# A two-layer convolution and DeltaNet backbone: TensorE issued in program order, four heads scanned together

## The chip, the cores and the metric

The kernel runs on one core of a Trainium2 chip. The metric is the device time of one launch in microseconds (us); three runs of the kernel before gave 2870.46, 2883.15 and 2887.36 us, and their median of 2883.15 us is the time to beat or lose to. The profile is of another execution of the same program; its time is known as the span from its first to its last instruction.

The engines named below: PE (TensorE, matrix multiply), DVE (VectorE), ACT (ScalarE), POOL (GpSimd), and SP (SyncE), whose queue issues every DMA of this kernel. Each works through its own list of instructions in order, and waits at an instruction until what it needs is there.

## The reference

Two layers over 256 context and 2048 latent tokens of width 1024. Per layer, cut to what matters:

```python
h = rms_norm(x, norm_w) * (1 + scale) + shift          # scale, shift, gate from silu(c) @ w_mod + b_mod
p = h @ w_in                                           # 1024 -> 4112 columns, float32
# group A: gated short convolution
ya = bg * conv(cg * xa) * silu(za)
# group B: q, k, v = silu(conv(.)), l2 norms, write gate beta, decay g; 4 heads of 128
a_mat = strict(beta * (k @ k.T) * decay)               # per chunk of tokens
sol = triangular_solve(a_mat + I, [v * beta, k * beta * exp(gcum)])
# scan over the chunks, forward and backward, latent scans start from the context's final state
u = u0 - w @ S
S = S * exp(g_last) + k_dec.T @ u
o = q_dec @ S + p_intra @ u
yb = rms_norm(o_forward + o_backward) * silu(zb)
x = x + gate * (concat(ya, yb) @ w_out)
```

The second layer's context is only read; after it comes a last `rms_norm`.

## The kernel before

**Tiling.** Tokens are 18 tiles of 128 (0 and 1 context, 2 to 17 latent), in chunks: chunk 0 is the context (256 tokens), chunks 1 to 4 are 512 latent tokens each. Float32 products are made of three passes: a tensor is split into a rounded part and a rest (`whi` and `wlo` of the weights, `h` and `l` of the tokens; `hc` and `lc` for chunk 0), and `project` (L272) sums `h·whi`, `l·whi` and `h·wlo` over 8 slices of the contraction. It does so in two halves of 256 columns (L276 to L278), each half with all 24 passes. One unit is 128 output columns: its weights are loaded (512 KB), rounded on ACT (L251) and subtracted on POOL (L253). A projected unit is consumed by ACT and DVE: convolution, SiLU, store to DRAM.

**Stages of a layer.** `prep` (L215) turns a chunk's normalised tokens channel-major: PE transposes into a PSUM bank (L225), ACT evicts with the modulation into `hf` (L231), DVE and POOL split it. In the same loop L240 projects the 16 gate columns in plain float32. Chunks 0 to 2 are also kept in DRAM (L233). `phase` runs units over chunks: q, k, v of the context, then of chunks 1 and 2, then 3 and 4; then the other units of 3 and 4; then those of 1, 2 (and 0), reloaded. `delta` (L476) takes one head's 16 latent tiles: per item it reloads the tile, transposes q, k, v (L495), makes `k·[k q]` (L511) and multiplies by the decays into `U` (L512); then it inverts the triangular blocks (31 elimination steps of two DVE instructions, L573 and L575) and assembles them on PE (L601 to L638). Then the same head's scan runs (`step`, L666): forward and backward step by step in turn, each a chain PE L684 (`k·S`), DVE L686 (`r`), PE L689 (`V·r`), DVE L692 (`wk`), PE L694, DVE L703 (new state), with L712 and L713 for the output. Each step loads its operands (256 KB, L674), and its triangle masks are applied on POOL out of `U`, which stays in SBUF (L678, L709). The four heads come one after the other beside the units of chunks 3 and 4.

**Order.** Every engine's list, PE's among them, is set by a scheduler that simulates the program and takes at each moment the most urgent instruction whose inputs it believes ready; `urgent()` raises the priority. So scan matmuls, item matmuls and projection passes are interleaved one by one.

## Time and profile before

| | |
|---|---|
| timed runs | 2870.46, 2883.15, 2887.36 us |
| span of the profiled execution | 2868.8 us |
| PE busy | 2740.4 us (96%) |
| DVE, ACT, POOL busy | 1794.5, 1139.6, 1002.2 us |
| mean granted TensorE clock | 0.982 |
| DMA queue, share of 16 engines | 53.7% |

The profiled execution is known by its span alone; the median of the runs is 14.35 us longer, the fastest run 1.7 us. "Busy" of PE counts pipelined matmuls with modelled ends, so a busy PE can still issue at different rates; how far apart matmuls start is the better measure. The granted clock is 1.00 at 2.4 GHz and 0.5 at 1.2 GHz.

### The profile page before, as it was taken

How to read it: one execution, taken by the hardware profiler on the slowest of the kernel's cores; microseconds unless marked ns; L12 is line 12 of the kernel's file. 1: busy time of each engine (PE TensorE's matmuls, PEld its weight loads, DVE VectorE, ACT ScalarE, POOL GpSimd, SP SyncE). 2: the span in 40 equal slices, each digit the busy share in tenths (PEclk: the TensorE clock that was granted, in tenths of full speed). 3: DMA queues.
4: the chain of work that ended last, by engine and by line, in shares of the span. 5: the costliest groups of instructions: out<-in, count | busy, mean ns of one | idle time of the engine just before them, and what ended most of it. 6: DMA issues, size and time to landing. Idle time of an engine off the chain costs nothing. (4 is left out here: it accounts for less than half of the span.)

```text
span 2868.8 us, 62580 instructions
## 1 busy us (share of the span) xinstructions
PE 2740.4 (96%) x23671; PEld 2529.1 (88%) x23671; DVE 1794.5 (63%) x4677; ACT 1139.6 (40%) x2962; POOL 1002.2 (35%) x1354
## 2 busy tenths in 40 slices
PE   7999999999999999999999999999999998999998
PEld 5799899988988999997777998899999888899887
DVE  5686657576586585353246776675766765754765
ACT  3544453533534532232115444435335354322332
POOL 2332322333433343234444222313334333333443
PEclk9999999999999999999999999999999999999999
DMA  8844265553655553347757552545546556434654
GB/s 275 251 120 138 81 174 130 174 162 89 182 145 170 173 139 113 109 149 246 239 161 242 162 144 79 154 112 163 154 115 188 132 168 189 126 116 118 206 173 117
DMA packets 589449, 450.17 MB, mean 157 GB/s; under 512 B 105322, under 2 KB 527196, under 8 KB 589148
## 3 DMA queue, kind: packets, MB, share of 16 engines
q1 hardware_dynamic: 589148, 446.16, 53.7%
q8 instruction: 188, 3.08, 0.4%
q14 instruction: 113, 0.93, 0.1%
HBM read 326.35 MB, written 119.70 MB: 155 GB/s over the span
## 5 line engine op out<-in xcount | busy, mean ns | idle before, releaser
L278 PE MATMUL pd<-h,whi 128*128 128x256 f32 x4096 | 1206.6, 295 | 2.1 <-ACT whi L251 2.1
L278 PE MATMUL pd<-l,whi 128*128 128x256 f32 x4096 | 1207.2, 295 | 0.0
L278 PE MATMUL pd<-h,wlo 128*128 128x256 f32 x4096 | 1199.4, 293 | 0.5 <-POOL wlo L253 0.5
L278 PEld LDWEIGHTS pd<-h,whi 128*128 128x128 f32 x4096 | 795.2, 194 | 11.9 <-issue 6.6
L278 PEld LDWEIGHTS pd<-l,whi 128*128 128x128 f32 x4096 | 795.0, 194 | 9.0 <-issue 5.4
L278 PEld LDWEIGHTS pd<-h,wlo 128*128 128x128 f32 x4096 | 794.8, 194 | 6.4 <-issue 2.9
L253 POOL TENSOR_TENSOR wlo<-raw,whi 128x1024 fp32r<-128x1024 f32 (+1 forms) x148 | 341.3, 2307 | 382.3 <-ACT whi L251 349.7
L899 PE MATMUL pd<-who,yy 128*128 128x512 f32 x1088 | 350.7, 397 | 0.4 <-ACT who L841 0.4
L899 PEld LDWEIGHTS pd<-who,yy 128*128 128x128 f32 x1088 | 203.6, 189 | 48.0 <-ACT yy L874 2.9
L697 ACT ACTIVATE w<-pscan,cs 128x128 f32<-128x128 f32 x272 | 99.5, 367 | 291.8 <-DVE wk L692 209.1
L899 PE MATMUL pd<-wlo,yy 128*128 128x512 f32 x544 | 214.1, 393 | 0.0
L251 ACT CAST whi<-raw 128x1024 fp32r<-128x1024 f32 x148 | 154.7, 1045 | 97.4 <-PE pd L278 60.9
L501 POOL TENSOR_TENSOR nk<-nk,phalf 128x1 f32<-128x1 f32 x144 | 81.7, 567 | 225.2 <-DVE nk L500 205.8
L573 DVE TENSOR_TENSOR tmp<-L,X 64x31 f32<-64x31 f32 (+15 forms) x310 | 127.1, 410 | 39.9 <-DMA L<-blk 25.0
L388 ACT ACTIVATE pd<-y 128x512 f32<-128x512 f32 (+1 forms) x116 | 65.5, 565 | 213.0 <-DVE y L288 200.6
L686 DVE SCALAR_TENSOR_TENSOR r<-pscan,eg,rc 128x128 f32<-128x128 f32 x272 | 93.7, 346 | 76.7 <-PE pscan L684 74.5
L575 DVE TENSOR_TENSOR X<-X,tmp 64x31 f32<-64x31 f32 (+15 forms) x310 | 136.3, 440 | 5.6
L692 DVE TENSOR_SCALAR wk<-pscan,cs 128x128 f32<-128x128 f32 x272 | 93.5, 346 | 69.6 <-PE pscan L689 67.7
L875 POOL TENSOR_TENSOR yy<-ys,yy 128x512 fp32r<-128x512 f32 x68 | 89.9, 1323 | 125.4 <-ACT yy L874 118.3
L660 POOL TENSOR_TENSOR so<-so,mhalf 128x1 f32<-128x1 f32 x136 | 79.2, 590 | 142.5 <-DVE so L659 134.3
L703 DVE SCALAR_TENSOR_TENSOR Sn<-Sn,atot,pscan 128x128 f32<-128x128 f32 x240 | 82.0, 342 | 67.9 <-PE pscan L694 66.6
L874 ACT CAST yy<-ys 128x512 fp32r<-128x512 f32 x68 | 42.1, 619 | 198.2 <-DVE ys L867 136.8
(2212 smaller groups left out, 5317.3 us busy)
## 6 DMA issues: line engine op xcount, KB each, us to landing
raw<-in_w_in_dram SPq DMA_DIRECT2D x148, 512.0 KB, 4.8
rc<-rec_d SPq DMA_DIRECT2D x272, 256.0 KB, 3.1
rec<-rec_d SPq DMA_DIRECT2D x136, 192.0 KB, 2.6
wm<-in_w_mod_dram SPq DMA_DIRECT2D x24, 1024.0 KB, 7.3
rec_d<-y SPq DMA_DIRECT2D x96, 256.0 KB, 2.9
rows<-row_d SPq DMA_DIRECT2D x144, 128.0 KB, 4.1
rec_d<-rec SPq DMA_DIRECT2D x144, 128.0 KB, 4.0
ys<-y_d SPq DMA_DIRECT2D x68, 256.0 KB, 3.5
```

Of the source, the lines that this page charges most:

```text
L251: nc.scalar.copy(hi, raw)
L253: eng.tensor_sub(lo[:, k], raw[:, k], hi[:, k].bitcast(F32))
L278: nc.tensor.matmul(acc[:, c:c + CW], w[i][:, k, :], h[j][:, k, c:c + CW], start=(z == 0), stop=(z == len(passes) - 1))
L501: nc.gpsimd.tensor_tensor(nk[:, i:i + 1], nk[:, i:i + 1], phalf[:, 0:1], ALU.pow)
L573: nc.vector.tensor_tensor(t3, L3[:, j + 1:32, j:j + 1].to_broadcast([2 * nb, m, k]), X3[:, j:j + 1, 0:k].to_broadcast([2 * nb, m, k]), ALU ...
L575: nc.vector.tensor_sub(X3[:, j + 1:32, 0:k], X3[:, j + 1:32, 0:k], t3)
L686: nc.vector.scalar_tensor_tensor(r, p1[:, 0:128], eg[:, g, col], vn, ALU.mult, ALU.subtract)
L692: nc.vector.tensor_scalar(wk, p2[:, 0:128], cs[:, 5 + z0 + d, i:i + 1], None, ALU.mult)
L697: nc.scalar.activation(w, p2[:, 0:128], AF.Copy, scale=cs[:, z0 + d, i:i + 1])
L703: nc.vector.scalar_tensor_tensor(Sn, S, atot[:, g, col], p3[:, 0:128], ALU.mult, ALU.add)
L875: nc.gpsimd.tensor_sub(l_, yr, h_.bitcast(F32))
L899: nc.tensor.matmul(acc, yy[k // 4][:, k % 4, :], wo[k][part][:, cs_], start=(z == 0), stop=(z == 23))
```

## The change

PE's list is no longer the scheduler's: it is the order in which the program emits instructions (`manual_schedule` for PE). The other engines are scheduled as before. The program is written as jobs (generators). `phase` emits projections, and after every three passes `pump` lets one due job emit a piece. A job that has emitted something says with `yield` how many microseconds of counted PE work are to go by before its next piece: 4.5 (`HOP`) between the links of a scan, 3.2 between items, 50 + 2 per item before the solved blocks are used, 1.3 between blocks of `prep`, and so on. `until` lets jobs emit without projections between when something named has to exist first.

The work changes too. `project` runs all 512 columns of a chunk in one matmul. The gate columns are projected in three-pass form (`two`). `delta` prepares two heads with 8 tiles each, and stores `U` to DRAM beside q, k, v. The scan is apart from it: one step takes all 4 heads of a tile, forward over all 16 tiles and then backward, its operands of 4 heads loaded in one transfer (128 x 3072 floats, 1536 KB, into a ring of two), masked in place on POOL; the backward pass adds the stored forward result. The scans of the latent tokens run beside the later units and the output projection. The edges of a phase with several chunks take three units chunk by chunk, so their weights are loaded once per chunk: 202 loads where there were 148. PSUM banks are fixed and taken in turn, and buffers come from rings; `hf` now has two buffers where it had four or five.

In the excerpts below PE's rows are in the order in which it issues them; a row with x4 is four such instructions. First a scan beside projections: the kernel before, in the first layer's units of chunks 1 and 2 or later (`pd` is a projection's bank, `pscan` a scan's).

```order
L278 MATMUL pd<-l,whi 128x256
L684 MATMUL pscan<-Sn,rc 128x128
L278 MATMUL pd<-h,wlo 128x256
L278 MATMUL pd<-h,whi 128x256
L278 MATMUL pd<-l,whi 128x256
L278 MATMUL pd<-h,wlo 128x256
L278 MATMUL pd<-h,whi 128x256
L662 MATMUL pscan<-ident,o_12043 128x128
L278 MATMUL pd<-l,whi 128x256
L694 MATMUL pscan<-wk,rc 128x128
L278 MATMUL pd<-h,wlo 128x256
L278 MATMUL pd<-h,whi 128x256
```

The change, two links of a scan step (`c_86` and `c_87` are the scan's banks, `d_81` and `d_82` a projection's):

```order
L149 MATMUL d_81<-h,whi 128x512
L149 MATMUL d_81<-l,whi 128x512
L149 MATMUL d_81<-h,wlo 128x512
L149 MATMUL c_86<-wk,rc 128x128 x4
L149 MATMUL c_87<-w,rc 128x128 x4
L149 MATMUL d_82<-h,whi 128x512
L149 MATMUL d_82<-l,whi 128x512
L149 MATMUL d_82<-h,wlo 128x512
L149 MATMUL d_82<-h,whi 128x512
```

Where single matmuls of one head stood among passes of 256 columns, four heads stand together among passes of 512; between the group before (`c_87<-r,rc`) and `c_86<-wk,rc` there are 24 projection rows, in the output stage mostly 21.

Second, where the first layer's q, k, v of chunks 1 and 2 end and chunk 3 is prepared (`xx` are its normalised tokens, `t_84`, `t_85` and `pt` the banks of transposes and items). Before, its transposes stand among projections:

```order
L278 MATMUL pd<-h,whi 128x256
L278 MATMUL pd<-l,whi 128x256
L278 MATMUL pd<-h,wlo 128x256
L278 MATMUL pd<-h,whi 128x256
L225 MATMUL pt<-ident,xx 128x128 x4
L689 MATMUL pscan<-rc,V__1719 128x128
L689 MATMUL pscan<-rc,V__1739 128x128
L278 MATMUL pd<-l,whi 128x256
L278 MATMUL pd<-h,wlo 128x256
L278 MATMUL pd<-h,whi 128x256
L278 MATMUL pd<-l,whi 128x256
```

In the change the last two projection rows of chunk 2 come first, and behind them items (`rec`) and the context's scan without a projection between:

```order
L149 MATMUL d_82<-l,whi 128x512
L149 MATMUL d_82<-h,wlo 128x512
L156 MATMUL t_84<-ident,rec 128x128 x3
L149 MATMUL t_85<-rec 128x256
L156 MATMUL t_84<-ident,rec 128x128 x3
L149 MATMUL t_85<-rec 128x256
L149 MATMUL c_87<-r,rc 128x128 x4
L156 MATMUL t_84<-ident,rec 128x128 x3
L149 MATMUL t_85<-rec 128x256
L149 MATMUL c_86<-wk,rc 128x128 x4
L149 MATMUL c_87<-w,rc 128x128 x4
L156 MATMUL t_84<-ident,rec 128x128 x3
```

This goes on to the end of the context's scan, and straight behind it come the blocks of chunk 3, eight in a row:

```order
L149 MATMUL c_86<-wk,rc 128x128 x4
L149 MATMUL c_87<-w,rc 128x128 x4
L156 MATMUL o_88<-ident,op 128x128 x8
L156 MATMUL t_84<-ident,xx 128x128 x4
L156 MATMUL t_85<-ident,xx 128x128 x4
```

Then chunk 3's projections begin. So from row 1068 to row 1100 of PE's list there is no projection.

The diff, cut to its core:

```diff
+HOP = 4.5
...
-    def stage(shape, n):
-        if n == 2:
-            return dp.tile(shape, F32, tag="rc", bufs=5, name="hf")
-        return dp.tile(shape, F32, tag="m2", bufs=4, name="hf")
...
+    def side(shape, name):
+        return dp.tile(shape, F32, tag="hf", bufs=2, name=name)
...
+    def mm(o, a, b, start=True, stop=True):
+        n = b.shape[-1]
+        nc.tensor.matmul(o, a, b, start=start, stop=stop)
+        if b.dtype == F32R:
+            Order.now += 0.0135 + n / 2400.0
+        else:
+            Order.now += 0.223 * n / 128 if n > 64 else 0.22 * n / 128 if a.shape[0] > 64 else 0.02
...
+    def spawn(name, gen):
+        Order.jobs.append([Order.now, gen, name])
+
+    def advance(job):
+        try:
+            d = next(job[1])
+            job[0] = Order.now + (d or 0.0)
+        except StopIteration:
+            Order.jobs.remove(job)
+            done.add(job[2])
+
+    def pump():
+
+        for job in Order.jobs:
+            if job[0] <= Order.now:
+                advance(job)
+                return
+
+    def until(what):
+
+        while what not in done:
+            job = min(Order.jobs, key=lambda j: j[0])
+            Order.now = max(Order.now, job[0])
+            advance(job)
 
     def vectors(l, P):
...
 
     def project(w, h):
-        W = h[0].shape[-1]
-        acc = pd()[:, 0:W]
-        passes = [(k, i, j) for k in range(KT) for i, j in ((0, 0), (0, 1), (1, 0))]
-        for c in range(0, W, CW):
-            for z, (k, i, j) in enumerate(passes):
-                nc.tensor.matmul(acc[:, c:c + CW], w[i][:, k, :], h[j][:, k, c:c + CW], start=(z == 0), stop=(z == len(passes) - 1))
+        acc = pd()[:, 0:h[0].shape[-1]]
+        for k in range(KT):
+            for z, (i, j) in enumerate(((0, 0), (0, 1), (1, 0))):
+                mm(acc, w[i][:, k, :], h[j][:, k, :], start=(k + z == 0), stop=(k + z == KT + 1))
+            if k < KT - 1:
+                pump()
         return acc
 
     def conv(dst, src, w, segs):
-        """dst = segment convolution of src, w the three per-channel weights."""
+
...
+            if xs is None:
+                xs = tokens_in(L, p)
+                yield 12.0
...
+                for k2 in range(0, KT, 2):
+                    ps = pt()
...
+                    hf = side([128, 2, 256], "hf")
...
+                    yield 1.3
+        done.add(("h", L.l, p))
...
+            yield 2.0
+            acc = pd()
+            for k in range(KT):
+                for j in range(2):
+                    mm(acc[0:96, 0:W], L.bw[:, 32 * k:32 * k + 96], L.hs[p][j][:, k, :], start=(k + j == 0), stop=(k + j == KT))
...
+    def phase(L, units, chunks, after, edge=3, ready={}):
+
+        N = len(units)
+        if len(chunks) == 1:
+            tasks = [(j, chunks[0]) for j in range(N)]
+        else:
+            tasks = [(j, p) for p in chunks for j in range(edge)]
+            tasks += [(j, p) for j in range(edge, N - edge) for p in chunks]
+            tasks += [(j, p) for p in chunks for j in range(N - edge, N)]
+        w = dict(ready)
+        left = {j: len(chunks) for j in range(N)}
+        of = {p: N for p in chunks}
+
+        def need(j):
+            if j < N and j not in w:
+                w[j] = weights(w_in[L.l], units[j][0], len(chunks) == 1)
+        for t, (j, p) in enumerate(tasks):
+            need(j)
+            wj = w[j] if t + 1 < len(tasks) and tasks[t + 1][0] == j else w.pop(j)
+            until(("h", L.l, p))
+            nxt = next((i for i, _ in tasks[t + 1:] if i != j), None)
+            if nxt is not None:
+                need(nxt)
+            a = project(wj, L.hs[p])
+            with urgent():
+                units[j][1](p, a)
+            left[j] -= 1
+            of[p] -= 1
+            for what, n in ((("unit", j), left[j]), (("chunk", p), of[p])):
+                if n == 0 and what in after:
+                    after[what]()
+            pump()
...
+            if i + 1 < n:
+                load(i + 1)
+            rec, rows = cur.pop(i)
+            with urgent():
                 tp = pt()
                 for s in range(s0, 3):
-                    nc.tensor.transpose(tp[:, 128 * s:128 * s + 128], rec[:, 3 - s, :], ident)
+                    turn(tp[:, 128 * s:128 * s + 128], rec[:, 3 - s, :])
+                kp = pt()
...
+            yield 3.2
+        held.discard("items")
...
+        yield 50.0 + 2.0 * n
...
+                    nc.sync.dma_start(out=L.rec_d[g:g + k, :, h, 512:512 + 128 * w_].rearrange("g p t -> p g t"),
+                                      in_=uz[:, j - i0:j - i0 + k, 0:w_, :].rearrange("p g s t -> p g (s t)"))
...
+                rc = dp.tile([128, NH, 6, 128], F32, tag="rc", bufs=2, name="rc")
+                if with_out:
+                    nc.sync.dma_start(out=rc.rearrange("p h s t -> p (h s t)"), in_=L.rec_d[g].rearrange("p h t -> p (h t)"))
...
+                for h in hd:
+                    m = rc[:, h, 4:4 + w_, :]
+                    nc.gpsimd.affine_select(out=m, in_=m, pattern=[[0, w_], [1 - 2 * d, 128]], compare_op=ALU.is_ge, fill=0.0, base=0, channel_multiplier=2 * d - 1)
...
+                    p1 = pscan("c0")
+                    for h in hd:
+                        mm(at(p1, h), kT[h], S[:, h, :])
+                    for h in hd:
+                        nc.vector.scalar_tensor_tensor(r[:, h, :], at(p1, h), e_(L.eg, h), vn[h], ALU.mult, ALU.subtract)
+                    if with_out:
+                        qs = pscan("o")
+                        for h in hd:
+                            mm(at(qs, h), qT[h], S[:, h, :])
...
+            yield HOP
+            with urgent():
+                p2 = pscan("c1")
+                for h in hd:
+                    mm(at(p2, h), V_[h], r[:, h, :])
+                wk = w4("wk")
+                for h in hd:
+                    nc.vector.tensor_scalar(wk[:, h, :], at(p2, h), cs(2 + d, h), None, ALU.mult)
...
+            yield HOP
+            with urgent():
+                p3 = pscan("c0")
+                for h in hd:
+                    mm(at(p3, h), kn[h], wk[:, h, :])
...
+                    pw = pscan("c1")
+                    for h in hd:
+                        mm(at(pw, h), P_[h], w[:, h, :])
...
+        def ready(g):
+            until(("y", l, g))
+            with urgent():
+                return mixed(g)
...
+        phase(L, [qkv_unit(L, s, h) for s, h in heads], (1, 2),
+              {("unit", 5): job(0), ("unit", 11): job(1), ("chunk", 1): lambda: spawn("p3", chunk_job(L, 3, False, z2))})
+        spawn("p4", chunk_job(L, 4, False, z2, last=True))
...
+        lat = list(range(2, NG))
+        w8 = {g: (f"J{l}3",) for g in range(10, NG)}
+        w8[2] = (f"J{l}1", f"C{l}0", f"C{l}1")
+        wb = {NG - 1: (f"F{l}0", f"J{l}3")}
+        spawn("lat", in_turn((f"F{l}0", alone("rc", scan(L, 0, lat, 0, wants=w8))), (f"F{l}1", alone("rc", scan(L, 1, lat[::-1], 1, wants=wb)))))
...
+    with tc.manual_schedule(engines={mybir.EngineType.PE}):
+        constants()
+        L = layers[0]
```

## Rows read from the trace of the kernel before

**Rows 1.** The page: busy us (share of the span) and instructions of each engine.

```profile
PE 2740.4 (96%) x23671; PEld 2529.1 (88%) x23671; DVE 1794.5 (63%) x4677; ACT 1139.6 (40%) x2962; POOL 1002.2 (35%) x1354
```

**Rows 2.** Span and mean granted TensorE clock of the core.

```profile
core 0: 2868.8 us, clock 0.982
```

**Rows 3.** Stretches with one kind of matmul: length, PE busy (matmuls), clock, DMA.

```profile
165.50:225.50 60.00, 60.00 (x502) 1.00 0.38 105
1498.70:1520.10 21.40, 21.40 (x96) 1.00 0.48 130
```

**Rows 4.** Timeline of PE in an output tile: start, length, matmuls.

```profile
1499.74 0.62 PE L899 MATMUL pd<-who,yy 128*128 128x512 f32 x2
1500.43 0.62 PE L899 MATMUL pd<-who,yy 128*128 128x512 f32 x2
```

**Rows 5.** PE groups: shapes, count | busy us, mean ns | idle before.

```profile
L278 PE MATMUL pd<-l,whi 128*128 128x256 f32 x4096 | 1207.2, 295 | 0.0
L240 PE MATMUL pt<-hf,braw 128*32 128x256 f32 x160 | 35.9, 390 | 0.3 <-ACT hf L231 0.3
L240 PE MATMUL pd<-hf,braw 128*32 128x256 f32 x128 | 30.6, 390 | 0.0
```

**Rows 6.** Timeline of PE: scan matmuls of one head amid projection.

```profile
1208.81 0.39 PE L694 MATMUL pscan<-wk,rc 128*128 128x128 f32 x2
1209.03 0.39 PE L713 MATMUL pscan<-w,P__11986 128*128 128x128 f32 x2
```

**Rows 7.** Waits of PE: us in total, times, longest.

```profile
PE pt L495 <- DMA rec<-rec_d: 20.0, 17, 3.6
PE pt L601 <- DMA tf<-blk: 14.2, 6, 3.4
PE pscan L684 <- DVE Sn L703: 14.0, 15, 2.8
PE pscan L689 <- DVE r L686: 11.4, 9, 3.3
PE pd L278 <- ACT whi L251: 5.0, 4, 2.1
PE pscan L684 <- DMA rc<-rec_d: 4.8, 2, 2.9
```

**Rows 8.** The page's costly groups on DVE, POOL and ACT.

```profile
L253 POOL TENSOR_TENSOR wlo<-raw,whi 128x1024 fp32r<-128x1024 f32 (+1 forms) x148 | 341.3, 2307 | 382.3 <-ACT whi L251 349.7
L251 ACT CAST whi<-raw 128x1024 fp32r<-128x1024 f32 x148 | 154.7, 1045 | 97.4 <-PE pd L278 60.9
L501 POOL TENSOR_TENSOR nk<-nk,phalf 128x1 f32<-128x1 f32 x144 | 81.7, 567 | 225.2 <-DVE nk L500 205.8
L686 DVE SCALAR_TENSOR_TENSOR r<-pscan,eg,rc 128x128 f32<-128x128 f32 x272 | 93.7, 346 | 76.7 <-PE pscan L684 74.5
```

**Rows 9.** Groups by line on ACT: a transposed block's eviction, and a token tile's squares.

```profile
L231 ACT ACTIVATE hf<-pscan,mod,am 128x256 f32<-128x256 f32 x80 | 40.1, 569 | 11.5 <-PE pscan L225 8.0 <-DVE am L150 1.4 <-issue 1.2
L183 ACT ACTIVATE junk<-xx 128x1024 bf16<-128x1024 f32 x28 | 29.8, 1065 | 36.3 <-DMA xx<-in_ctx_dram 23.4 <-DMA rec_d<-rec 4.9 <-DMA xx<-in_x_dram 3.4
```

**Rows 10.** DMA issues: count, KB each, median us to landing.

```profile
raw<-in_w_in_dram SPq DMA_DIRECT2D x148, 512.0 KB, 4.8
wm<-in_w_mod_dram SPq DMA_DIRECT2D x24, 1024.0 KB, 7.3
xx<-x SPq DMA_DIRECT2D x29, 512.0 KB, 4.9
h_d<-hf SPq DMA_DIRECT2D x36, 256.0 KB, 5.6
```

**Rows 11.** One line, the scan's triangle mask: ns minimum/median/maximum, first and last start.

```profile
L678 POOL TENSOR_SCALAR_AFFINE_SELECT V__1719<-U x1: 292/292/292, 250.2 to 250.2; 128x128 f32<-128x128 f32 x1
```

**Rows 12.** Timeline of DVE: last item of a head is prepared.

```profile
425.47 0.36 DVE L512 TENSOR_TENSOR U<-pt,dm 128x256 f32<-128x256 f32 x1
```

**Rows 13.** Timeline of PE: first matmul on that head's solved blocks.

```profile
497.31 0.25 PE L601 MATMUL pt<-tf,U 32*32 32x32 f32 x4 [3.18 <-DMA tf<-blk]
```

More of the change, by code (lines that the diff above doesn't have):

```diff
@@ new lines, in hybrid_backbone_kernel, with alone @@
+    class Order:
+        now = 0.0
+        jobs = []
+    done = set()
+    held = set()
+    def alone(what, gen):
+        while what in held:
+            yield 1.0
+        held.add(what)
+        yield from gen
+        held.discard(what)
+    def mm(o, a, b, start=True, stop=True):
[5 more added lines that the diff above has]
+            Order.now += 0.223 * n / 128 if n > 64 else 0.22 * n / 128 if a.shape[0] > 64 else 0.02
@@ L383, in consume, with mix_units, unit @@
+    def mix_units(L, a_, chunks):
+        par = L.P["par"]
+        cw = [par[:, 32 + 4 * j + a_:33 + 4 * j + a_] for j in range(3)]
+        t0 = {}
+        o = 0
+        for ci in chunks:
+            t0[ci] = o
+            o += 128 * CHUNKS[ci][1]
+        def unit(u):
             def consume(ci, a):
@@ L474, in layer @@
[L474 to L492 removed]
+                xs = xa[:, t0[ci]:t0[ci] + W]
@@ new lines, in delta, with load @@
+    def delta(L, items, with_out, before):
+        n = len(items)
+        heads = list(dict.fromkeys(h for h, _ in items))
+        nh, m = len(heads), n // len(heads)
+        h0, g0 = heads[0], items[0][1]
+        gs = slice(g0, g0 + m)
+        U = []
+        cur = {}
+        ssk = dp.tile([128, 16], F32, tag="ssk", bufs=2, name="ssk")
+        nk = dp.tile([128, 16], F32, tag="nk", bufs=2, name="nk")
+        s0 = 0 if with_out else 1
+        w_ = 2 if with_out else 1
+        def load(i):
+            with urgent():
+                h, g = items[i]
+                rec = small([128, 4, 128], "rec")
+                nc.sync.dma_start(out=rec[:, 1:4 - s0].rearrange("p s t -> p (s t)"), in_=L.rec_d[g, :, h, 128:512 - 128 * s0])
+                rows = dp.tile([128, 2, 128], F32, tag="rows", bufs=2, name="rows")
+                nc.sync.dma_start(out=rows, in_=L.row_d[8 * g + h:8 * g + h + 5:4].partition_broadcast(128))
+                cur[i] = rec, rows
+        while "items" in held:
+            yield 1.0
+        held.add("items")
+        load(0)
+        yield 6.0
+        for i, (h, g) in enumerate(items):
+            if i == 8 and before is not None:
+                while before not in done:
+                    yield 2.0
+            if i % 8 == 0:
+                U.append(dp.tile([128, 8, 2, 128], F32, tag="u", bufs=3, name="U"))
+            if i + 1 < n:
+                load(i + 1)
+            rec, rows = cur.pop(i)
+            with urgent():
@@ new lines, in hybrid_backbone_kernel @@
+    with tc.manual_schedule(engines={mybir.EngineType.PE}):
+        constants()
+        L = layers[0]
+        with urgent():
+            vectors(0, L.P)
+            xs0 = tokens_in(L, 0)
+            tables(L)
+            wm = []
+            for n in range(8):
+                if n % 2 == 0:
+                    wt = hp.tile([128, KT, 512], F32, tag="hl"[n // 2 % 2], bufs=2, name="wm")
+                wm.append(wt[:, :, CW * (n % 2):CW * (n % 2) + CW])
+                mod_load(0, wm[n], 2 * n)
+            for n in range(8):
+                for _ in mod_piece(0, L.P, wm[n], 2 * n):
+                    pass
+            mod_scale(0, L.P)
+        L.ready = {j: weights(w_in[0], qkv_unit(L, s, 0)[0], True) for j, s in enumerate((1, 2))}
+        spawn("p0", chunk_job(L, 0, True, {}, xs=xs0, last=True))
+        layer(L, layers[1])
+        until("next")
+        layer(layers[1], None)
```

1226 lines of the change are left out of this document (605 added, 621 removed).

## The prediction, made before the changed kernel ran

> **What bounds the kernel now.** I read the page's list of engines first: PE is busy 96% of the span and has four times as many instructions as the next engine [rows 1]. The view of the core shows the TensorE clock granted at 0.982 of full speed [rows 2]. So the kernel is bound by PE's list, and its time has three parts: what PE does, 128.4 us in which it idles (2868.8 - 2740.4) [rows 1, 2], and about 52 us that the clock kept back (0.018 x 2868.8) [rows 2]. A busy DVE or POOL matters only where PE waits for it.
>
> Then I looked at how far matmuls stand apart, in stretches that hold one kind alone. In 60 us of projection with 256 columns there are 502, 0.1195 us each; in 21.4 us of output projection with 512 columns there are 96, 0.223 each; both at clock 1.00 [rows 3]. The timeline has three 512-wide ones in 0.69 us, 0.23 each [rows 4]. I take 0.227 for a whole chunk, with 0.223 and 0.230 as ends. Two halves cost 0.239.
>
> Last, the waits. The six that cost PE most add up to 69.4 us: items that wait for their reload, solved blocks for their way through DRAM, and the links of a scan for DVE [rows 7].
>
> **The change part by part.** The base is the profiled execution's span, 2868.8 us; the median of the runs is 14.35 longer, and I add that at the end.
>
> Projection: three groups of 4096 matmuls, one of which is shown [rows 5], are 12288 halves x 0.1195 = 1468 us; 6144 whole ones x 0.227 = 1395. That is -74 (-55 at 0.230, -98 at 0.223).
>
> The Trainium skill ("TensorE: Matmul & The Clock Gate", section "Back-to-back issue gap") gives a warm matmul N/2.4 + 2.5 ns. By it a pair saves only the 2.5 ns, 6144 times 15 us, not 74. The rows here disagree: 119.5 ns is 12.8 above 256/2.4, so the part that does not grow with the columns is larger in this kernel than on that page [rows 3].
>
> Gate columns: 288 float32 matmuls are busy for 66.5 us [rows 5]. In three passes, run as two per slice, there are 128 of 512 columns and 32 of 256: 128 x 0.227 + 32 x 0.1195 = 33. That is -27, after some 6 for what they still stand beside (0 to -34).
>
> Scan matmuls: four heads in step need 16 more than before, counted in PE's list, at 0.22 each [rows 6]: +3.5.
>
> Waits that go: a scan's links come 21 or 24 projection passes apart, 21 x 0.227 = 4.8 us. The chain between them is a matmul of 0.39 [rows 6] and four DVE instructions of 0.346 [rows 8], 1.8 us. So DVE's part (14.0 + 11.4) goes. Items are loaded one ahead (20.0). Solved blocks are planned 82 us behind the last item; before they took from 425.47 to 497.31, 71.8 us [rows 12, 13], so 14.2 goes too, and so does 4.8 for `rc` [rows 7]. That is 64.4; smaller waits of these kinds lie in the rest of the 128.4. I take -75 (-30 if items and blocks stay late, -105 if nearly all idle time goes). L278's wait for rounded weights (5.0) stays.
>
> Clock: part of the 52 us follows such waits. I take -30 (0 to -45).
>
> What is late next are the borders where one chunk must be ready before PE has anything to project. Chunk 3's tokens share buffers with the context's scan, which ends directly ahead of them. Then come a token load of 4.9 [rows 10], two squares of 1.065 with the scaling behind them, about 3, and eight blocks of two evictions of 0.569, 9.1 [rows 9]. Of these 17 us some 7 lie beside the matmuls of items and scan: 10 a layer. Chunks 1 and 2 store each block from `hf`, a ring of two, and the store lands after 5.6 [rows 10]. Two blocks per 5.6 + 0.6 make 25 us for eight, where 10.4 are planned (8 x 1.3): 14 late per chunk. Projections of the chunk before cover most of it: I take 11 a layer. At the layers' border the gates' chain runs with little beside it: 15, from the same loads and evictions. Sum 2 x 10 + 2 x 11 + 15 = +57. Ends: 25 if the borders overlap with items, 140 if nothing covers them (2 x 17 + 4 x 14 + 50). A clock that falls in these gaps takes back +10 (0 to 40).
>
> Edges: the units that run chunk by chunk load 54 more weights (202 against 148), and then each weight serves 24 matmuls, 5.45 us. ACT rounds in 1.045 and POOL subtracts in 2.307 [rows 8], behind a load of 4.8 [rows 10], one unit ahead. Hidden in the mean, with POOL's queue behind it: I take +15 (0, to 54 x 3.36 = 181 if nothing hides ACT and POOL).
>
> Items and blocks take turns in two transpose banks, and an item comes every 3.2 us and more. Its chain through DVE and POOL (0.567 for one small POOL step [rows 8]) is about 2 us. 144 items give 0 to 144 us; I take +10, near the lower end, since a projection group lies between most of them. The stores of `U`, its reload and the masks moved to the load lie off PE's path unless the rival below holds.
>
> Sum: -74 - 27 + 3.5 - 75 - 30 + 57 + 10 + 15 + 10 = -110. The span becomes about 2758, and with 14.35 the time **2773**.
>
> **The rivals.** *The borders are covered.* The pieces that jobs emit between them may fill them, and edges and banks may cost nothing: -110 - 67 - 25, and 15 more from the clock, is -217, hence 2666. For it speaks that PE's order then has few stalls of any other kind; against it that some 30 of PE's rows at chunk 3 are emitted without a projection, and that blocks go at ACT's pace [rows 9].
>
> *The wide matmul gains nothing.* If the passes of whole chunks come 0.239 apart, the sum is -36 and the time 2847. Against it: the rows of 512 columns are the same kind of matmul at the same clock, with a DMA share of 0.48 beside 0.38 [rows 3, 4]. For it: they stand in the output projection, and no row shows a unit of `project` at that width.
>
> *The scan's operands come late (the other side).* A step loads 1536 KB into a ring of two. 512 KB land after 4.8, 1024 KB after 7.3 [rows 10], so 1536 KB after about 9.8. Then POOL masks four heads of 256 columns, 0.58 each by 0.292 for 128 [rows 11], 2.3, perhaps behind a `wlo` of 2.3 [rows 8]: 14.4 in all. A step lasts 3 x 4.8 + 22 x 0.22 = 19.2, and the buffer comes free only when the step before has ended. That leaves 4.8 to spare. If loads queue on SP behind weights and DRAM stores by 9 us, each of 64 latent steps (2 layers, 2 directions, 16) is 4 late: +256, 3029. From 124/64 = 1.9 us late per step on the kernel is slower than before by more than can be told from no change. For it: DMA rises by 202 weight loads and the reloads of `U`, and PE's order, being fixed, can no longer do something else meanwhile. Against it: before, the queue waited little for anything that PE needed (4.8 us for `rc` [rows 7]).
>
> *Waits come back at the two transpose banks and at the items.* At 0.7 us for each of 144 items, 100 more: the sum is about -10 and the time 2873, no change. For it: the 20.0 for items was the greatest wait before [rows 7], in a list that could put anything ahead of it. Against it: the planned distance is longer than the chain.
>
> **How the numbers follow.** Forecast 0.48, its own range 2710 to 2835 (the terms' ends taken together, not all on one side); borders covered 0.25; nothing from width 0.05; operands late 0.12; waits back 0.10. A difference of 0.5%, 14.4 us, is about what can be told from no change here, so faster means under 2868.7 and slower over 2897.6. The first three cases are faster, 0.78; the waits' case is the same, 0.10; late operands slower, 0.12. The range goes from 2640, near the low end of covered borders, to 2890, above the waits' case, and leaves out the late operands and the tail of the second case.
>
> **What would show it.** In the profile after: 6144 projection matmuls of 512 columns, 0.227 apart in a stretch that holds only these; two halves' 0.239 would prove the second rival. PE's waits at `k·S` and `V·r` for DVE near zero, and for items and `tf` under 10 us; if a wait for `rc` or for its mask leads the list, the third rival holds. Idle time of PE should stand in a few gaps of 5 to 20 us, at the first projection of chunks 1 to 3 of each layer and at the layers' border, behind ACT's block evictions or the `hf` stores; many short gaps at items and transposes mean the fourth. The clock should be near 0.99. By the sum PE's busy time falls by about 118 (-74 - 27 + 3.5 - 30 + 10) and its idle time rises to about 135 (128.4 - 75 + 57 + 15 + 10). The forecast is wrong in its mechanism if busy time falls by less than 60, or if idle time lies outside 90 to 200.

## The result and the profile after

The changed kernel takes 3189.04 us in the median of four runs (3182.18 to 3192.17) and the kernel before 2882.68 in four: a ratio of 1.107 (95% interval 1.104 to 1.110). It is slower by 306 us, where 110 us less were forecast. The view of the core and the page's list of engines, against [rows 1, 2]:

```profile
core 0: 3189.0 us, clock 0.924
...
PE 2715.6 (85%) x17431; PEld 2245.5 (70%) x17431; DVE 1667.2 (52%) x3988; ACT 1209.0 (38%) x3112; POOL 1072.1 (34%) x1069
```

PE has 6240 fewer matmuls. Its work no longer fills its time: it idles 473.4 us (3189.0 - 2715.6) where it idled 128.4. Its clock fell with it. From the clock's records, worked out from the trace: PE was busy at 1.2 GHz for 289.7 us, before for 93.0, and half of such time is counted as lost, since the granted clock in these records is 0.5. So the difference of the two spans, 320.2 us, is

- idle time: 473.4 - 128.4 = +345.0
- clock lost while busy: (289.7 - 93.0) / 2 = +98.3
- PE's work at full clock: -123.1, what remains (2715.6 - 289.7/2 against 2740.4 - 93.0/2)

What PE stood in front of is read from its groups by shape: busy us, mean ns | idle just before them, and what ended it.

```profile
L149 PE MATMUL d<-h,whi 128*128 128x512 f32 x2048 | 871.2, 425 | 86.7 <-ACT whi L301 80.1 <-DVE y L522 6.5
L149 PE MATMUL d<-h,wlo 128*128 128x512 f32 x2048 | 825.0, 403 | 18.4 <-POOL wlo L303 17.0 <-issue 1.4
L149 PE MATMUL d<-who,yy 128*128 128x512 f32 x1088 | 364.3, 404 | 17.8 <-ACT yy L975 16.0 <-ACT who L938 1.4 <-POOL yy L976 0.5
...
L156 PE MATMUL t<-ident,rec 128*128 128x128 f32 x424 | 79.2, 299 | 91.0 <-ACT rec L657 65.6 <-DMA rec<-rec_d 22.3 <-ACT hf L417 1.7
L156 PE MATMUL t<-ident,xx 128*128 128x128 f32 x288 | 60.2, 359 | 58.2 <-ACT hf L417 24.2 <-ACT rec L657 19.5 <-ACT v L758 9.0
L149 PE MATMUL t<-g_z,tri_u 128*128 128x64 f32 x8 | 2.4, 400 | 21.3 <-DVE g_z L475 21.3
```

In the kernel before, the groups like the first, fourth and fifth idled 2.1, 20.2 and 2.6 us:

```profile
L278 PE MATMUL pd<-h,whi 128*128 128x256 f32 x4096 | 1206.6, 295 | 2.1 <-ACT whi L251 2.1
L495 PE MATMUL pt<-ident,rec 128*128 128x128 f32 x424 | 73.4, 277 | 20.2 <-DMA rec<-rec_d 20.0
L225 PE MATMUL pscan<-ident,xx 128*128 128x128 f32 x144 | 25.9, 302 | 2.6 <-DVE xx L212 2.2 <-ACT hf L231 0.2
```

Summed over all groups of a kind, with g3 (below), the scheduled kernel with four edits, beside them:

| idle of PE ahead of | before | forecast | after | g3 |
|---|---|---|---|---|
| projections (weights, h) | 9.7 | +15 | 125.7 | 58.9 |
| items | 20.4 | -10 | 104.0 | 44.7 |
| blocks, gate columns, gates | 5.2 | +57 | 106.9 | 37.5 |
| solved blocks | 19.0 | -14 | 29.6 | 40.6 |
| scan | 50.3 | -30 | 49.8 | 42.8 |
| modulation, start | 15.0 | 0 | 29.5 | 25.0 |
| output | 0.4 | 0 | 19.7 | 41.0 |

Of the forecast, another -11 belonged to no one group. By place it is as uneven. Five stretches of the first layer (length, busy us of PE, PEld, DVE, ACT, POOL, clock, DMA share, GB/s):

```profile
250.00:460.00 210.00, 150.53 (x1195) 121.61 (x1197) 131.49 (x344) 109.76 (x320) 66.49 (x80) 0.82 0.59 175
910.00:1000.00 90.00, 52.46 (x526) 39.67 (x527) 28.71 (x37) 28.84 (x37) 21.82 (x12) 0.73 0.42 114
1000.00:1340.00 340.00, 336.75 (x2153) 296.14 (x2148) 130.88 (x321) 106.98 (x283) 113.21 (x118) 1.00 0.55 176
1340.00:1420.00 80.00, 38.99 (x209) 33.45 (x208) 27.68 (x49) 24.16 (x53) 29.16 (x24) 0.73 0.62 195
1420.00:1690.00 270.00, 260.52 (x1428) 210.09 (x1426) 88.96 (x197) 52.83 (x157) 114.37 (x107) 0.99 0.62 194
```

In the third and fifth the pipeline does what it was written for: scans of four heads beside projections or output matmuls, PE at 96 to 99%. In none of the five is DVE busy over 63%, and ACT and POOL are below 53%. PE is not displaced by a busier engine; it waits for chains. A clock that shows where time goes is the moment at which PE has issued so many thousand columns of projection and output matmuls (4227 in all, the same in both), worked out from the trace:

| columns | before at us | after at us | g3 at us |
|---|---|---|---|
| 200 | 187.5 | 228.1 | 210.9 |
| 400 | 329.7 | 450.6 | 389.6 |
| 600 | 445.8 | 599.7 | 500.1 |
| 1000 | 747.8 | 870.6 | 775.0 |
| 1600 | 1191.9 | 1268.6 | 1209.4 |
| 2200 | 1514.9 | 1673.9 | 1547.1 |
| 2600 | 1793.0 | 2088.4 | 1899.4 |
| 3600 | 2528.7 | 2750.8 | 2498.7 |
| 4227 | 2859.8 | 3180.4 | 2966.4 |

Up to 600 thousand, the first layer's q, k, v of the context, of chunks 1 and 2 and of most of 3 and 4, 154 us are lost, 121 of them up to 400; to 1600, 77 are won back; to 2200, the first layer's last units and its output, 82 are lost; in the second layer's first stretch, 2200 to 2600, 136 more; to 3600, 73 are won back; and at its end 98 are lost. Not all of that is idle time: a stretch is longer too when more matmuls of the scan stand in it, as in the last one, with 808 after and 366 before.

Two places. At the border to chunk 3 (PE's timeline) three pieces in 24 us each stand 4 to 6 us, for ACT's last read of a bank and for DVE, and no projection stands between them:

```profile
351.92 0.90 PE L156 MATMUL t<-ident,rec 128*128 128x128 f32 x3 [5.63 <-ACT rec L657]
357.93 1.22 PE L149 MATMUL t<-rec 128*128 128x256 f32 x2 [5.12 <-DVE U L652]
...
369.64 0.55 PE L156 MATMUL t<-ident,rec 128*128 128x128 f32 x3 [3.79 <-ACT rec L657]
```

And where the units of chunks 3 and 4 give way to reloaded chunks, a unit's weights stand behind a reload (PE, ACT and SP, each its own timeline):

```profile
986.54 0.79 PE L149 MATMUL d<-h,whi 128*128 128x512 f32 x1 [17.87 <-ACT whi L301]
```

```profile
978.88 1.04 ACT L301 CAST h<-raw 128x1024 fp32r<-128x1024 f32 x1 [5.78 <-DMA raw<-h_d]
982.23 1.04 ACT L301 CAST h<-raw 128x1024 fp32r<-128x1024 f32 x1 [2.31 <-DMA raw<-h_d]
985.45 1.04 ACT L301 CAST whi<-raw 128x1024 fp32r<-128x1024 f32 x1 [2.17 <-DMA raw<-in_w_in_dram]
```

```profile
961.64 6.76 SPq L963 DMA_DIRECT2D ys<-y_d  x2
974.89 0.36 SPq L300 DMA_DIRECT2D raw<-h_d  x1
```

Reload and weights pass through the same two `raw` buffers, in turn; and ahead of them SP stood 12.9 us with two early loads for the output (`ys`), which waited for buffers of the solved blocks:

```profile
SPq L963 <- PE t L149: 6.9, 1, 6.9
SPq L963 <- DVE vf L761: 6.0, 1, 6.0
```

### The profile page after: what moved, and what is told of

The parts are those of the page before. It is cut to its first block, busy times and chain, and to the rows that moved or that the text cites. A ratio compares the mean times of both kernels' runs of the same rounds, so it can differ in the third digit from the quotient of the medians.

```text
span 3189.0 us, 48188 instructions
## 1 busy us (share of the span) xinstructions
PE 2715.6 (85%) x17431; PEld 2245.5 (70%) x17431; DVE 1667.2 (52%) x3988; ACT 1209.0 (38%) x3112; POOL 1072.1 (34%) x1069
## 5 line engine op out<-in xcount | busy, mean ns | idle before, releaser
L149 PE MATMUL d<-h,whi 128*128 128x512 f32 x2048 | 871.2, 425 | 86.7 <-ACT whi L301 80.1
L149 PE MATMUL d<-h,wlo 128*128 128x512 f32 x2048 | 825.0, 403 | 18.4 <-POOL wlo L303 17.0
L149 PE MATMUL d<-l,whi 128*128 128x512 f32 x2048 | 821.7, 401 | 0.0
L149 PEld LDWEIGHTS d<-h,whi 128*128 128x128 f32 x2048 | 400.7, 196 | 174.0 <-ACT whi L301 83.8
L149 PEld LDWEIGHTS d<-h,wlo 128*128 128x128 f32 x2048 | 398.4, 195 | 113.7 <-POOL wlo L303 24.3
L149 PEld LDWEIGHTS d<-l,whi 128*128 128x128 f32 x2048 | 400.6, 196 | 76.8
L149 PE MATMUL d<-who,yy 128*128 128x512 f32 x1088 | 364.3, 404 | 17.8 <-ACT yy L975 16.0
L149 PEld LDWEIGHTS d<-who,yy 128*128 128x128 f32 x1088 | 207.5, 191 | 66.4 <-ACT yy L975 16.2
L149 PE MATMUL d<-wlo,yy 128*128 128x512 f32 x544 | 214.8, 395 | 1.8 <-DVE wlo L939 1.8
L711 DVE TENSOR_TENSOR tmp<-Lt,X 64x31 f32<-64x31 f32 (+15 forms) x310 | 129.8, 419 | 26.8 <-DMA Lt<-blk 20.8
L713 DVE TENSOR_TENSOR X<-X,tmp 64x31 f32<-64x31 f32 (+15 forms) x310 | 128.4, 414 | 6.0
```

The source lines that it names most:

```text
L149: nc.tensor.matmul(o, a, b, start=start, stop=stop)
L711: nc.vector.tensor_tensor(t3, L3[:, j + 1:32, j:j + 1].to_broadcast([2 * nb, m_, k]), X3[:, j:j + 1, 0:k].to_broadcast([2 * nb, m_, k]), A ...
L713: nc.vector.tensor_sub(X3[:, j + 1:32, 0:k], X3[:, j + 1:32, 0:k], t3)
```

## The experiments

Times are medians of four runs, beside the kernel before on the same chip (2871 to 2878 us). The changed kernel's 3189.04 was taken beside 2882.68, so a difference to it is sure to some 12 us only. "Idle" is PE's, from one profile each.

**e1_scheduled_pe.** How much is the fixed order?

```diff
-    with tc.manual_schedule(engines={mybir.EngineType.PE}):
+    with nullcontext():
```

> The changed program, but PE's list is made by the scheduler as in the kernel before; all else (wide passes, 4 heads in step, rings, edges, stores of U) stays. Theory A, the fixed order is what costs: PE waits at an item, a chunk's blocks or gates while projections that could run stand behind them; the scheduler would pull these ahead. Then PE's idle time falls from 473 us to under 200 and the time to 2700-2850. Rival B, the program itself (two transpose banks, a ring of two for hf, three units at an edge whose weights come one ahead) is late in whatever order: idle time stays above 350, time 3050-3300.

3091.24 us, idle 381. So in this program the order alone costs 98 us, and the larger part, some 210, is in the program as it stands. Rival B holds: PE still waits 58.3 for weights and 41.0 for blocks.

**e2_before_wide.** The wide pass alone, in the kernel before.

```diff
-        for c in range(0, W, CW):
-            for z, (k, i, j) in enumerate(passes):
+        for z, (k, i, j) in enumerate(passes):
```

> The kernel before with one edit: projections in one matmul of a chunk's whole width. By the pitch of 0.227 against 2 x 0.1195 that the two traces show, 6144 x 0.012 = 74 us less: about 2810. If the scheduler's waits grow because its grains are coarser, less is gained: 2840-2880.

2958.53 us, slower by 88 (ratio 1.030, 1.028 to 1.032). It met neither expectation. Projections run ahead, and at the ends of the layers the four heads' scans are left, link after link: PE's idle ahead of scan matmuls is 103 us, 50 before. Three stretches, all matmuls first, then those of projection alone (length, busy us of PE and of PEld, clock):

```profile
930.00:1076.00 146.00, 140.40 (x1184) 120.55 (x1183) 77.15 (x222) 54.63 (x163) 50.03 (x78) 0.98 0.41 114
1076.00:1320.00 244.00, 210.42 (x1469) 174.46 (x1468) 149.68 (x469) 80.57 (x228) 77.50 (x157) 0.84 0.51 152
2569.00:2843.00 274.00, 229.21 (x1467) 186.60 (x1466) 182.11 (x549) 97.54 (x278) 96.65 (x191) 0.81 0.55 160
```

```profile
930.00:1076.00 146.00, 110.93 (x491) 80.96 (x492) 0.98 0.41 114
1076.00:1320.00 244.00, 90.14 (x406) 64.90 (x405) 0.84 0.51 152
2569.00:2843.00 274.00, 18.19 (x69) 12.23 (x67) 0.81 0.55 160
```

At 1600 thousand columns this kernel was 115 us ahead of before (1076.4 against 1191.9), at 1800 it was 10 behind. In the last stretch only 18 of 229 busy us are projection and 87 output, and the clock is at 0.81. This fits that in the kernel before the scans in sequence last nearly as long as the work beside them, and that less of that work does not shorten them.

**f5_before_wide_where_no_scan.** The same for chunks 0 to 2 only.

```diff
-                a = project(w[j], hs[p])
+                a = project(w[j], hs[p], p < 3)    # whole width if true
```

> The kernel before, with whole-width passes for chunks 0 to 2 alone: 3072 of 6144 pairs, at stages where no scan of the latent tokens should run beside them. If the wide pass was slow in the kernel before only because the four heads' scans in sequence then lack projections beside them, half the width term remains: 2876 - 37 = 2839, idle as before. If scans still run beside these chunks, or the coarser grain itself costs, 2870-2920.

2922.19 us, slower by 44 (ratio 1.017, 1.014 to 1.019). PE's idle ahead of scan matmuls is 85 us here, 50 before, so scans do run beside these chunks. As in e2 the kernel is ahead of before until late in each layer, 27 us at 1600 thousand columns and 22 at 3600, and behind it at the end, where more scan is left. Whether the coarser grain costs something by itself stays open.

**e3_narrow.** The width's term in the changed kernel.

```diff
-                mm(acc, w[i][:, k, :], h[j][:, k, :], ...)
+                for c in range(0, W, CW):
+                    nc.tensor.matmul(acc[:, c:c + CW], w[i][:, k, :], h[j][:, k, c:c + CW], ...)
```

> The changed kernel with each whole-width pass cut into two halves of 256 columns, in the same place of PE's list. If the width term was sized right (74 us) the time is 3189 + 74 = 3263, idle time about as before. If the longer list fills waits that are fixed by other engines, part of it vanishes in idle time: 3200-3240.

3234.03 us, 45 more than 3189.04. Its PE:

```profile
PE 2782.9 (86%) x23575; PEld 2604.9 (81%) x23575; DVE 1667.0 (52%) x3988; ACT 1211.1 (37%) x3112; POOL 1070.3 (33%) x1069
```

PE is busy 67.3 us longer (2782.9 - 2715.6), 60 of them at full clock, and idles 21 less. The term of 74 was near; a third of what PE saves turned into waiting. The Trainium skill ("TensorE: Matmul & The Clock Gate", section "Back-to-back issue gap") gives N/2.4 + 2.5 ns for a warm matmul by itself. By it the 6144 cuts would cost an estimated 15 us; the trace does not agree.

**e4_context_scan_later.** Take the context's scan out of the border to chunk 3.

```diff
-(f"C{l}0", alone("rc", scan(...)))
+(f"C{l}0", later(("h", l, 4), alone("rc", scan(...))))   # begins when chunk 4 is prepared
```

> The changed kernel, with the context's scan held back until chunk 4 of the layer is prepared, so that chunk 3's tokens do not wait for its buffers and PE's list has no stretch of items and scan alone. Theory A': that stretch (310 to 430 us in layer 0, 1960 to 2070 in layer 1) costs some 50 to 60 us of idle time a layer and a low clock beside it; then the time falls by 60 to 140 us, to 3050-3130. Rival: items and blocks pay the same waits wherever they stand: within 30 us of 3189.

3222.73 us, 34 slower. At 400 thousand columns it was 53 us ahead (397.1 against 450.6), at 1400 it was 8 behind (1161.1 against 1153.2). PE's idle falls by 11 ahead of items, but rises by 20 ahead of the scan, 10 ahead of blocks and gates and 7 ahead of projections. The theory fails; the rival's range, within 30 us, is missed by 4, so that the waits only move is near but not shown.

**e5_split_in_dram.** Reloads without `raw`, ACT and DVE; stores that leave `hf` alone.

```diff
-                        nc.sync.dma_start(out=L.h_d[p][:, k2:k2 + 2, o], in_=hf)
+                        nc.sync.dma_start(out=L.h_d[p][:, k2:k2 + 2, o], in_=h_.bitcast(F32))
+                        nc.sync.dma_start(out=L.l_d[p][:, k2:k2 + 2, o], in_=lo[:, k2:k2 + 2, o].bitcast(F32))
...
-                    split(L.h_d[p][:, k:k + 4, o:o + 256], hi, lo, ((nc.vector, slice(0, 4)),))
+                    nc.sync.dma_start(out=t[:, k:k + 4, :].bitcast(F32), in_=t_d[:, k:k + 4, :])   # t: hi, lo
```

> The changed kernel, but the two rounded parts of a chunk's tokens are kept in DRAM instead of their sum: the store no longer reads hf, and a reload is four DMAs straight into the tiles, with no raw buffer, no rounding on ACT and no subtraction on DVE. Theory: the ring of two hf held by stores and the reloads that share the raw buffers and ACT with weights cost PE what its waits at blocks of chunks 1 and 2 and at whi behind a reload show, together some 80 to 110 us with the low clock behind them: 3080-3140. Rival: the blocks wait for ACT and the weights for POOL and SP in any case: 3160-3200.

3116.9 us, 72 less, and the wait for `whi` is halved:

```profile
PE d L149 <- ACT whi L301: 46.8, 10, 11.5
```

Nearly all of it comes at reloads: at 1000 thousand columns it stands at 873.1 (after 870.6), at 1200 it is 33 ahead, and most of the rest comes between 3200 and 3400, the second layer's reload. In the changed kernel `hf` was held by its store, but not for long: ACT waited for it 8 times, 15.9 us in all, since a store lands after 2.4 us, not the 5.6 of [rows 10] (a wait of ACT: us, times, longest; the store: count, KB, median us to landing).

```profile
ACT hf L417 <- DMA h_d<-hf: 15.9, 8, 3.6
```

```profile
h_d<-hf SPq DMA_DIRECT2D x36, 256.0 KB, 2.4
```

Without it PE's idle ahead of the blocks falls from 58.2 to 41.6, yet up to 1000 thousand columns no time is won. The two halves of the edit were not run apart.

**e6_longer_distances.**

```diff
-            yield 9.0     # gates; blocks 1.3, items 3.2, solved blocks 50 + 2n
+            yield 20.0    # gates; blocks 2.2, items 4.5, solved blocks 70 + 2n
```

> The changed kernel with more counted PE work between the pieces of jobs: gates 20 us for 9, blocks 2.2 for 1.3, items 4.5 for 3.2, solved blocks 70 + 2 per item for 50 + 2. Theory: pieces come earlier in PE's list than their inputs; then waits at items, gates and solved blocks go down by half, idle time by 80 to 100, time to 3070-3120. Rival: where nothing else may run (until a chunk is ready) a distance is not filled by anything, and elsewhere the pieces now come late for those who need them: 3180 or slower.

3222.07 us, 33 slower. Idle ahead of gates fell from 38.0 to 19.6 and of items from 104.0 to 87.7, but rose from 49.8 to 88.3 ahead of the scan and from 29.6 to 45.8 ahead of solved blocks. So the waits moved.

**e7_three_transpose_banks.**

```diff
-             for k, n in (("d", 3), ("t", 2), ...)}
+             for k, n in (("d", 2), ("t", 3), ...)}
```

> The changed kernel with three PSUM banks for transposes, items, gates and blocks, and two for projections (two and three before). Theory: the waits of transposes for ACT's last read of rec and hf are waits for one of two banks; they go from about 135 us to under 60, and the time to 3100-3140, if two projection banks suffice (a unit lasts 5.45 us, ACT and DVE read it in about 3). Rival: the operands are what comes late, or projections now wait for their bank: 3180-3260.

3255.17 us, 66 slower: the third bank helped where it came, items from 104.0 to 76.2, blocks, gate columns and gates from 106.9 to 59.2, solved blocks from 29.6 to 12.9, and projections paid more for theirs, until DVE had read a bank:

```profile
PE d L149 <- DVE y L522: 137.5, 40, 9.7
```

**e8_edge_six** and **f1_split_edge_one.**

```diff
-    def phase(L, units, chunks, after, edge=3, ready={}):
+    def phase(L, units, chunks, after, edge=6, ready={}):    # f1: edge=1, on top of e5
```

> The changed kernel with six units instead of three taken chunk by chunk at the edges of a phase. Theory: at an edge a chunk's preparation (17 to 25 us) has 16 us of projections beside it, and with six units 33; the waits at borders go, the weights that are loaded more often are hidden: 3090-3150. Rival: weights that serve one chunk come late (ACT, POOL and a raw ring of two at 5.45 us per unit), then more edge is worse: 3210-3300, with whi and wlo waits up.

> The kernel with the tokens' two parts in DRAM (3117 us), and one unit instead of three taken chunk by chunk at the edges. Theory: six units at an edge made it 122 us slower since each more weight load brings ACT, POOL and a raw buffer into a unit of 5.45 us; with one the load count falls by 36 and the time by 30 to 60, to 3055-3090. Rival: the edges are needed as cover for the next chunk's preparation, and one unit of 5.45 us covers less: 3120-3180.

With six, 3311.44 us, 122 slower. Its weight loads, and its waits for ACT and POOL (us, times, longest), against 92.0 and 18.6 after:

```profile
raw<-in_w_in_dram SPq DMA_DIRECT2D x256, 512.0 KB, 4.8
```

```profile
PE d L149 <- ACT whi L301: 100.6, 12, 16.1
...
PE d L149 <- POOL wlo L303: 38.2, 27, 3.9
```

The waits for weights rise by 28 us, and PE's idle ahead of items and of solved blocks by 23 and 29, so the next 54 loads are only part of the 122. With one, 148 loads as before the change, and 3096.72 us, 20 less than e5. The forecast's +15 for 54 loads was near.

**f2_split_edge_one_scheduled.** f1 with e1's edit.

> The same, with PE's list made by the scheduler. If program order and edges are separate causes, another 98 us as in the run with the scheduled list: 2960-2990. If the scheduler already took the time that the edges cost, less: 3030-3080.

3073.13 us: 24 less than f1, not 98. The gains overlap.

**f3_items_free_bank_early.** An item's transposes are copied out of the bank before POOL's root; v is scaled in SBUF.

```diff
-                nc.scalar.copy(rec[:, 0, :], tp[:, 128:256])
-                nc.scalar.activation(rec[:, 1, :], tp[:, 256:384], AF.Copy, scale=nk[:, i:i + 1])
+                nc.scalar.copy(rec[:, 0:2, :], tp[:, 128:384])      # ahead of nk, as two slices
+                nc.scalar.activation(rec[:, 1, :], rec[:, 1, :], AF.Copy, scale=nk[:, i:i + 1])
```

> The changed kernel, in which an item's transposes are copied out of their bank as soon as their squares are taken, and v is scaled later in SBUF: one chain less (DVE, POOL, ACT) before the bank is free. Theory: transposes wait for the last read of the bank because it stands behind POOL's root; the 86 us of waits at ACT rec fall to 30-45 and the time to 3120-3150. Rival: ACT is late for other reasons (its list puts the copies late): the waits move to the new copy, time within 20 of 3189.

3164.73 us, 24 less. PE's wait of transposes for that read falls from 85.7 to 26.9, but idle ahead of items only from 104.0 to 93.4: the next link was late (`rec`'s reload 34.0, DVE's `U` 22.5).

**g1_preparation_on_scan_banks, g2_all_in_program_order, g3_all_scheduled.**

```diff
-                    ps = pt()                                        # a chunk's blocks
+                    ps = pscan(("c0", "c1")[k2 // 2 % 2])            # gate columns and gates alike
```

> The changed kernel, with a chunk's blocks, gate columns and gates in the scan's three PSUM banks, which the scan of the latent tokens does not use at that time, so that items and solved blocks have the two transpose banks to themselves. Theory: the ring of two banks, handed out in program order, chains items, blocks, gates and solved blocks to each other; with a third bank their waits fell by 90 us, and only the lack of a third projection bank ate that. Then 3190 goes to 3070-3110. Rival: these pieces wait for their own operands (ACT's evictions, loads, DVE's gate chain), or now for the context's scan, which has the same banks: 3150-3230.

> Together: banks apart, both parts of the tokens in DRAM, one unit at an edge, items that free their bank early; PE in program order. If the causes are separate, 3190 - 72 - 20 - 24 - 100 = about 2975. If the same idle time is counted in several, 3020-3080.

> The same with PE's list made by the scheduler. With banks apart the scheduler may move blocks ahead of items, which the common ring forbade: 2880-2950 if program order and the ring were the two halves of what is left. If the rest lies in chains through DRAM, ACT and DVE that no order hides, within 40 us of the run in program order.

g1: 3156.74, 32 less: idle ahead of blocks falls from 58.2 to 26.4, but of items rises from 104.0 to 116.8. g2, g1 with e5, f1 and f3: 3053.54, so the four together are worth 136, less than their sum of 148. g3: 2975.97, another 78. That is 213 of the 306 us, and still 100 over before (ratio 1.036, 1.033 to 1.039):

```profile
core 0: 2975.1 us, clock 0.944
...
PE 2676.4 (90%) x17431; PEld 2225.1 (75%) x17431; DVE 1621.8 (55%) x3970; ACT 1141.9 (38%) x3040; POOL 948.2 (32%) x1015
```

**g4_context_scan_later_scheduled** (g3 with e4's edit) and **g5_output_order** (g3, the first layer's output beginning with two latent tiles instead of the context's two).

```diff
-            tiles = [0, 1] + tiles
+            tiles = tiles[0:2] + [0, 1] + tiles[2:]
```

> All edits and the scheduled list, and the context's scan held back until chunk 4 is prepared. In program order alone this made the kernel 34 us slower. Theory: chunk 3's tokens get their buffers earlier and a scheduler uses it: 2930-2960. Rival: the waits only move with the scan, as before: 2970-3010.

> All edits and the scheduled list (2976 us), and the first layer's output takes two latent tiles ahead of the two context tiles. Theory: the context tiles need the units projected last, so PE stands for the chain store, reload, product with the gate, rounding (19.9 us in one gap); with two other tiles ahead, whose units are long stored, the gap goes, and with it as much again of a low clock's half: 2950-2960. Rival: those tiles need the backward scan, which is then late: 2975-2990.

g5: 2970.03 (2962.95 to 2976.92), 6 less than g3 (2972.77 to 2985.12): the runs overlap. Idle ahead of output matmuls falls from 41.0 to 24.3, so the chain was there, and little of it reaches the end. g4: 3106.14, 130 slower than g3. One wait leads it:

```profile
PE t L149 <- DMA tf<-blk: 109.3, 7, 49.5
```

PE's list has the solved blocks' matmuls up to 49.5 us ahead of their data from DRAM, and all behind them waits. So an order made by a simulation can be wrong too.

## Why the prediction was wrong

**The step that failed is the idle time:** "its idle time rises to about 135". It rose to 473, and PE's busy time fell by 24.8 where about 118 were forecast; the prediction's own marks of a wrong mechanism (a fall of less than 60, idle outside 90 to 200) are both met. Three terms made the idle time, each about in the right place and much too small, and one was missing:

- *Items and transposes in two banks.* The prediction bounded them by 0 to 144 us and took 10, "near the lower end, since a projection group lies between most of them". Idle ahead of items is 104.0, 84 more than before. Where a chunk must be ready next, no projection lies between: a list in program order lets items and scan go by there one after the other; 47 of the 104 stand in the two borders to chunk 3 (310 to 430 and 1960 to 2070 us). f3 takes 59 of the 86 us that transposes wait for the bank's last read, and gains 24: the next link takes much of its place.
- *The 64 us of waits "that go".* Those for `r` and `Sn` did go: PE's waits for DVE `S` and for `r` are 1.0 and 0. But idle ahead of the scan stayed at 49.8 against 50.3, at other links (`wk` 15.4, `w` 10.8, a step's scaled output 14.1). For items and solved blocks the distances counted in work are not distances in time: `until` sets the program's clock ahead where PE has nothing else. That they cost time for this reason is argued from the code; e6 only shows that longer ones do not help.
- *Borders.* +57 was forecast and 101.7 more measured ahead of blocks, gate columns and gates. Of the reasons given, `hf` held by its store was real and small: 15.9 us of ACT's time (e5). g1 points to the bank that blocks share with items.
- *Reloads were no term at all.* With weights they share two raw buffers, ACT and SP. So they did in the kernel before (18 loads `raw<-h_d` in either trace), where PE idled 9.7 us ahead of all projections. e5 makes reloads and stores 72 us, the largest cause that a run isolated but for program order (e1). Why they come late now is not isolated: e1, with its list scheduled, still waits 58.3 for weights.

Clock: -30 + 10 was forecast, +98.3 came. It goes with the idle time: in the five stretches above it is 0.73 and 0.82 where PE idles 28 to 51%, and 0.99 or 1.00 where it is busy over 96%.

**What was right.** PE's work: -97.5 for the three terms, -123.1 measured, though in part because errors cancel: by the time from one start to the next, at full clock, projections fell by 134 (74 forecast), of which e3 gives the width 60; gate columns fell by 24 (27), and the scan's matmuls rose by 37 (3.5) and the items' by 13 (0). The pitch of a whole-width pass was taken as 0.227; 17 passes beside a scan in the timeline are 3.89 us, 0.229 each, between these two:

```profile
1102.05 0.39 PE L149 MATMUL d<-l,whi 128*128 128x512 f32 x1
...
1105.94 0.39 PE L149 MATMUL d<-h,whi 128*128 128x512 f32 x1
```

So the second rival fails. Edges: +15 taken, 20 measured on top of e5. The third rival, late operands, fails in its mechanism though its sign was the one that came: `rc` cost PE 2.1 us, and 1536 KB land sooner than the estimate of 9.8:

```profile
rc<-rec_d SPq DMA_DIRECT2D x68, 1536.0 KB, 7.3
```

The fourth rival, waits come back at banks and items, named a mechanism that came, with a chance of 0.10. Its 100 us is near the 84 at items, but it had none of the reloads, the borders or the clock. One reading of the page was off, with no term behind it: PE has five times as many instructions as DVE [rows 1], not four.

**The deeper fault** was to count waits by the kernel before. Its list was made so that something ready stood ahead of nearly every wait. [rows 7] show what was left after that, not what the chains cost. Taking the scheduler away lays them open; e1 gives 98 us for that, g3 78 on top of the other edits, f2 24. And the program was written with fewer ways around: tokens share buffers with the scan, and one ring of two banks holds four kinds of pieces. The kernel before had the blocks of chunks 0 to 2 in the scan's banks (`pscan<-ident,xx` in its trace), as g1 has all of them.

**What stays open.** g3 is 100 us slower than before with PE's work 130 us smaller. Its idle is 299 (before 128) and its busy time at 1.2 GHz 224 us (93). No row dominates. By the clock of columns it is 54 us behind at 600 thousand and loses 74 between 2200 and 2600, but at 3600 it is 30 ahead, and the largest loss, 137 us, is the second layer's end: 1024 scan matmuls are left there where the kernel before has 366, and PE idles 44 us more. That looks like e2, the scan left at the end, but no run here changes it alone. Whether stores and reloads of `U`, the solver's round trip, or the tokens' ring carry the rest, no run here tells. Nor was the scan in step tried in the kernel before, so its own worth is not isolated.

## What to carry to other kernels

The waits in a profile of a scheduled kernel are what the scheduler could not hide. If a change takes the reordering away, price each chain by its whole length from issue to use, and ask at each border which independent work stands in the list between. Two things that take turns in one ring, of PSUM banks or of staging buffers, are one chain in an in-order list; look for such rings ahead of counting matmuls. And a faster matmul is worth something only while the chain beside it still has cover: a third of the saving vanished here, and in the kernel before all of it and more.

## What the runs showed that was not expected

Whole-width passes, cheaper by 67 us of PE time in the changed kernel, made the kernel before 88 us slower. Moving each layer's four-step context scan cost 34 us in program order and 130 with a scheduler (e4, g4). Six units chunk by chunk at the edges, in place of three, cost 122 us, of which 28 are waits for weights; one in place of three saved 20.
